# Finer pieces at the opening of an 8x8 max-pool-and-subtract kernel on Trainium2

## Chip, cores, metric

The kernel runs on one core of one Trainium2 chip. The metric is the device time of one execution, in microseconds, lower being better. Of seven executions of the kernel before, the median was 628.34 us (628.24 to 628.9).

## What is computed

The input `x` is float32 of shape 8 x 64 x 256 x 256 (134.22 MB). Each image is cut into blocks of 8 by 8 elements; from every element the maximum of its block is subtracted. The output has the shape of the input.

```python
x_r = x.reshape(B, C, oH, pH, oW, pW)          # pH = pW = 8
pooled = x_r.max(axis=(3, 5))
upsampled = np.repeat(np.repeat(pooled, pH, axis=2), pW, axis=3)
return (x - upsampled).astype(np.float32)
```

## The kernel before

One "row" here is eight image lines of one channel, 8 x 256 = 2048 float32 (8 KB): a row holds 32 whole blocks, and so every row can be worked on alone. There are 8 x 64 x 32 = 16,384 rows, 128 for each of the 128 partitions. The list `TILES` (L11) says how these 128 rows per partition are divided: 32 tiles of four rows each. Inside a tile a partition's rows stand next to each other in HBM (L69, L70), so a piece of one, two or four rows is one stretch of 8, 16 or 32 KB per partition, and 1, 2 or 4 MB over all partitions.

An entry of `TILES` is a pair of lists: the pieces in which a tile is loaded, and the pieces in which it is worked on and stored. Before, the first tile is loaded as two pieces of two rows and stored as two pieces of two rows; thirty tiles are loaded and stored as one piece of four rows; the last tile is loaded as one piece and stored as two, one and one rows.

For each tile the loop of L64 takes a buffer `dat` of 32 KB per partition (L65, from a pool of `BUFS` = 6 buffers) and a small one, `pooled`, for the maxima (L66). Then:

- each load piece is a DMA from `in_x_dram` into a slice of `dat`, issued from the SyncE queue (SP, L75);
- for each store piece VectorE (DVE) makes one TENSOR_REDUCE that takes the maxima of the piece's blocks into `pooled` (L41 where the piece has one row, L48 where it has more), then one TENSOR_TENSOR per row that subtracts them in place (L55), and then a DMA from `dat` to `out_dram` is issued from the ScalarE queue (ACT, L81).

All loads go through SP's DMA queue (q1 in the profile), all stores through ACT's (q10); both run on the same 16 DMA engines. TensorE is not used, and ScalarE and SyncE only issue DMAs. The order on each engine is the program's order (`manual_schedule`, L62). The waits come from the tile framework: DVE waits for the load piece it reads; a store waits for DVE; a load into a buffer used before waits until the stores of the tile six places earlier have landed. The DMAs signal on eight semaphores handed out in turn, so that a DMA also waits for the earlier DMA which has the same semaphore.

Of the kernel before, what the change touches and what calls it, by code (L numbers as in the profile page):

```python
# [1 line left out]

# [4 lines left out]

F32 = mybir.dt.float32
ROW = 2048

TILES = [([2, 2], [2, 2])] + [([4], [4])] * 30 + [([4], [2, 1, 1])]  # L11
BUFS = 6


@with_exitstack
def kernel(
    ctx: ExitStack,
    tc: tile.TileContext,
    x: bass.AP,
    out: bass.AP,  # L20
):
    nc = tc.nc
    P = nc.NUM_PARTITIONS
    B, C, H, W = x.shape
    pH = pW = 8
    oW = W // pW

    x_rows = x.rearrange("b c (oh ph) w -> (b c oh) (ph w)", ph=pH)
    out_rows = out.rearrange("b c (oh ph) w -> (b c oh) (ph w)", ph=pH)
    assert sum(sum(loads) for loads, _ in TILES) * P == x_rows.shape[0]  # L30
    size = max(sum(loads) for loads, _ in TILES)

    data = ctx.enter_context(tc.tile_pool(name="data", bufs=BUFS))
    small = ctx.enter_context(tc.tile_pool(name="small", bufs=BUFS))

    def pool_and_subtract(dat, tops, R):

        wins = dat.rearrange("p (r ph ow pw) -> p r ph ow pw", r=R, ph=pH, ow=oW)
        tops = tops.rearrange("p (r ow) -> p r ow", r=R)
        if R == 1:  # L40
            nc.vector.tensor_reduce(  # L41
                out=tops[:, 0],
                in_=wins[:, 0].rearrange("p ph ow pw -> p ow ph pw"),
                axis=mybir.AxisListType.XY,
                op=mybir.AluOpType.max,
            )
        else:
            nc.vector.tensor_reduce(  # L48
                out=tops,
                in_=wins.rearrange("p r ph ow pw -> p r ow ph pw"),  # L50
                axis=mybir.AxisListType.XY,
                op=mybir.AluOpType.max,
            )
        for r in range(R):
            nc.vector.tensor_tensor(  # L55
                out=wins[:, r],
                in0=wins[:, r],
                in1=tops[:, r].unsqueeze(1).unsqueeze(3).to_broadcast([P, pH, oW, pW]),
                op=mybir.AluOpType.subtract,
            )  # L60

    ctx.enter_context(tc.manual_schedule())  # L62
    at = 0
    for loads, stores in TILES:  # L64
        dat = data.tile([P, size * ROW], F32, name="dat")  # L65
        pooled = small.tile([P, size * oW], F32, name="pooled")  # L66

        rows = sum(loads)
        src = x_rows[at : at + P * rows].rearrange("(p r) d -> p (r d)", r=rows)  # L69
        dst = out_rows[at : at + P * rows].rearrange("(p r) d -> p (r d)", r=rows)  # L70
        at += P * rows
        lo = 0
        for R in loads:
            part = slice(lo * ROW, (lo + R) * ROW)
            nc.sync.dma_start(out=dat[:, part], in_=src[:, part])  # L75
            lo += R
        lo = 0
        for R in stores:
            part = slice(lo * ROW, (lo + R) * ROW)
            pool_and_subtract(dat[:, part], pooled[:, lo * oW : (lo + R) * oW], R)  # L80
            nc.scalar.dma_start(out=dst[:, part], in_=dat[:, part])  # L81
            lo += R


# [1 line left out]
_INS = ['x']  # L86
_OUTS = [((8, 64, 256, 256), 'float32')]


# [23 lines left out]
```

## Time and profile before

| | |
|---|---|
| median of seven executions | 628.34 us |
| the profiled execution, its own time | 628.47 us |
| span from its first to its last instruction | 626.5 us |
| moved from and to HBM | 134.22 MB read, 134.22 MB written |
| mean rate over the span | 428 GB/s |
| VectorE | 562.6 us busy (90% of the span), 163 instructions |
| DMAs: loads | 31 of 4096 KB, 2 of 2048 KB |
| DMAs: stores | 30 of 4096 KB, 3 of 2048 KB, 2 of 1024 KB |
| TENSOR_REDUCE of four rows, two rows, one row (mean) | 8.685, 4.418, 2.278 us |
| TENSOR_TENSOR of one row (mean) | 2.287 us |

The profile is of one execution. 1.97 us of its time lie outside the span. Times inside it count from the start of the span. "DMA" in tables of windows is the mean busy share of the 16 DMA engines, and GB/s what they moved, reads and writes together; a packet is counted where it begins, so that short windows scatter around the true share.

### The profile page before, as it was taken

Reading aid. Unit: us, or ns where it says so; the run is one execution under the profiler, and the core shown is the slowest. Engines: PE = TensorE matmul, PEld = TensorE weight load, DVE = VectorE, ACT = ScalarE, POOL = GpSimd, SP = SyncE. Lnnn points to the kernel's source line nnn. Section 1 sums busy time; section 2 is a strip of 40 time slices with the busy share of each in tenths; the row PEclk is TensorE's granted clock in tenths of the full one; section 3 lists DMA queues with packets and bytes.
Section 4 is the critical chain, followed back from the end, with each engine's and each line's share of the span. In section 5 each row is a group of like instructions: output and inputs, shape, how many; then the busy total and the mean of one; then the engine's idle time right before and its main releaser. Section 6 shows DMA issues by size and latency. Waiting matters only on the chain.

```text
span 626.5 us, 364 instructions
## 1 busy us (share of the span) xinstructions
DVE 562.6 (90%) x163; POOL 0.2 (0%) x4
## 2 busy tenths in 40 slices
DVE  4999999998898888988889988889888898888982
POOL 0000000000000000000000000000000000000000
DMA  9999999999999999999999999999999999999997
GB/s 370 400 446 425 435 435 435 435 435 435 435 435 431 433 435 429 429 429 427 435 435 433 435 435 435 435 435 435 435 435 433 433 435 427 431 423 433 435 434 337
DMA packets 9794, 268.46 MB, mean 428 GB/s; under 512 B 1088, under 2 KB 1088, under 8 KB 1088
## 3 DMA queue, kind: packets, MB, share of 16 engines
q1 hardware_dynamic: 4752, 134.22, 49.9%
q10 hardware_dynamic: 5040, 134.22, 49.6%
q14 instruction: 2, 0.02, 0.0%
HBM read 134.22 MB, written 134.22 MB: 428 GB/s over the span
## 4 chain that ended last, share of the span: by engine, by line
DVE 90%; another core or an unknown queue 7%; DMA 1%; issue 0%
DVE dat L55 45%; DVE pooled L48 44%; DMA dat<-in_x_dram 1%; DVE pooled L41 1%
## 5 line engine op out<-in xcount | busy, mean ns | idle before, releaser
L48 DVE TENSOR_REDUCE pooled<-dat 128x128 f32<-128x8192 f32 (+1 forms) x33 | 273.8, 8297 | 51.3 <-DMA dat<-in_x_dram 51.3
L55 DVE TENSOR_TENSOR dat<-dat,pooled 128x2048 f32<-128x2048 f32 x128 | 285.0, 2287 | 1.2
L41 DVE TENSOR_REDUCE pooled<-dat 128x32 f32<-128x2048 f32 x2 | 4.6, 2278 | 0.0
L97 POOL MEMSET const-bfloat16-1.0<- 128x1 bf16 x1 | 0.1, 102 | 0.0
L97 POOL MEMSET const-uint8-127<- 128x1 uint8 x1 | 0.1, 102 | 0.0
L97 POOL MEMSET const-float32-1.0<- 128x1 f32 x1 | 0.1, 99 | 0.0
L97 POOL MEMSET const-float32-0.0<- 128x1 f32 x1 | 0.1, 98 | 0.2 <-issue 0.2
## 6 DMA issues: line engine op xcount, KB each, us to landing
dat<-in_x_dram SPq DMA_DIRECT2D x31, 4096.0 KB, 60.9
out_dram<-dat ACTq DMA_DIRECT2D x30, 4096.0 KB, 37.5
out_dram<-dat ACTq DMA_DIRECT2D x3, 2048.0 KB, 19.9
dat<-in_x_dram SPq DMA_DIRECT2D x2, 2048.0 KB, 9.5
out_dram<-dat ACTq DMA_DIRECT2D x2, 1024.0 KB, 11.2
```

The costliest lines, as they stand in the source:

```text
L41: nc.vector.tensor_reduce(out=tops[:, 0], in_=wins[:, 0].rearrange("p ph ow pw -> p ow ph pw"), axis=mybir.AxisListType.XY, op=mybir.AluOp ...
L48: nc.vector.tensor_reduce(out=tops, in_=wins.rearrange("p r ph ow pw -> p r ow ph pw"), axis=mybir.AxisListType.XY, op=mybir.AluOpType.max,)
L55: nc.vector.tensor_tensor(out=wins[:, r], in0=wins[:, r], in1=tops[:, r].unsqueeze(1).unsqueeze(3).to_broadcast([P, pH, oW, pW]), op=mybir ...
L97: nc = _bacc.Bacc("TRN2", target_bir_lowering=False, num_devices=1)
```

## The change

One line: the first tile is now loaded and stored in pieces of one, one and two rows; the second tile, which came in as one piece of four rows and left as one, is now loaded and stored in two pieces of two rows (as the first tile was before); 29 whole tiles instead of 30 follow, and the last tile is as it was.

```diff
-TILES = [([2, 2], [2, 2])] + [([4], [4])] * 30 + [([4], [2, 1, 1])]
+TILES = [([1, 1, 2], [1, 1, 2]), ([2, 2], [2, 2])] + [([4], [4])] * 29 + [([4], [2, 1, 1])]
```

The built programs show what this makes of each engine's instructions. SP issues two loads of 1024 KB, three of 2048 KB and 30 of 4096 KB, 35 in place of 33. ACT issues two stores of 1024 KB, three of 2048 KB and 29 of 4096 KB ahead of the last tile's three, 37 in place of 35. DVE opens with two one-row reductions (L41), each with its subtraction, then three two-row reductions (L48) with two subtractions each, where it had two two-row reductions and one of four rows: two reductions more, and the same number of subtractions. The semaphores handed out in turn fall on other DMAs: in the program before, the sixth and the seventh load wait for the landing of the first and the third load; in the changed one the sixth to the ninth load wait for the first, third, fourth and fifth. The buffers, the engines that issue and everything after the second tile are unchanged.

## Prediction

> **What bounds the kernel now.** I read the page first: busy shares, rates by slice, DMA queues.
>
> ```profile
> DVE 562.6 (90%) x163; POOL 0.2 (0%) x4
> ...
> DVE  4999999998898888988889988889888898888982
> ...
> DMA  9999999999999999999999999999999999999997
> GB/s 370 400 446 425 435 435 435 435 435 435 435 435 431 433 435 429 429 429 427 435 435 433 435 435 435 435 435 435 435 435 433 433 435 427 431 423 433 435 434 337
> DMA packets 9794, 268.46 MB, mean 428 GB/s; under 512 B 1088, under 2 KB 1088, under 8 KB 1088
> ```
>
> DVE has holes in nearly every slice behind the first quarter; the DMA engines are at nine tenths or more from the first slice on, the last one apart. The rate stands at 423 to 435 GB/s whatever DVE does. That is a full pipe, with the time set by bytes. The chain of waits seems to say otherwise, so it was read second, together with DVE's and SP's waits:
>
> ```profile
> DVE 90%; another core or an unknown queue 7%; DMA 1%; issue 0%
> ...
> DVE pooled L48 <- DMA dat<-in_x_dram: 51.3, 26, 8.0
> ...
> SPq L75 <- DMA out_dram<-dat: 501.4, 27, 19.7
> SPq L75 <- DMA dat<-in_x_dram: 21.3, 2, 16.3
> ```
>
> The chain runs along DVE because it is followed from instruction to instruction; but DVE itself waits 26 times for a load, 8.0 us at the start and 43.3 us in the other 25. The 7% named as unknown are mostly these waits, some 1.72 us before each whole tile. So DVE keeps step with the loads, and the loads with the full pipe. Third, windows, to find where the pipe is not full:
>
> ```profile
> 0.00:2.00 2.00, 0.00 (x0) 0.20 (x4) 1.00 0.47 98
> 2.00:4.00 2.00, 0.00 (x0) 0.00 (x0) 1.00 0.75 295
> 4.00:12.00 8.00, 3.97 (x1) 0.00 (x0) 1.00 0.99 426
> 12.00:18.00 6.00, 5.96 (x4) 0.00 (x0) 1.00 1.01 437
> 18.00:24.00 6.00, 5.96 (x3) 0.00 (x0) 1.00 0.98 350
> 24.00:60.00 36.00, 35.93 (x11) 0.00 (x0) 1.00 1.01 437
> 120.00:580.00 460.00, 417.61 (x121) 0.00 (x0) 1.00 1.00 433
> 613.00:619.00 6.00, 2.16 (x1) 0.00 (x0) 1.00 0.93 396
> 619.00:623.00 4.00, 0.00 (x0) 0.00 (x0) 1.00 1.01 428
> 623.00:625.00 2.00, 0.00 (x0) 0.00 (x0) 1.00 0.17 70
> ```
>
> (The last column is GB/s.) I take 433, the long window, as the full rate: 268.46 MB need 620.0 us of the 626.5. The missing 6.5 us lie at the start (0 to 4 us moved 0.79 MB, worth 1.8 us: 2.2 lost), at 18 to 24 us (350 instead of 433: 6 x 83/433 = 1.15 lost, at a DMA share of 0.98, so packets were slow there, not absent) and behind 613 (0.5, then 0.05, then 3.2 us from 623 to the end); the 437s give some 0.4 back. In between nothing is to be had. Loads alone, from 4 to 18 us, run at the same rate as loads and stores together: a store that begins earlier does not fill an empty pipe, it takes turns with a load.
>
> **The change, part by part.** *An earlier first result.* These lines show the start and the end before:
>
> ```profile
> 8.03 4.42 DVE L48 TENSOR_REDUCE pooled<-dat 128x64 f32<-128x4096 f32 x1 [8.03 <-DMA dat<-in_x_dram]
> 12.48 4.49 DVE L55 TENSOR_TENSOR dat<-dat,pooled 128x2048 f32<-128x2048 f32 x2
> ...
> 17.01 44.26 ACTq L81 DMA_DIRECT2D out_dram<-dat  x4
> ...
> 612.86 2.29 DVE L55 TENSOR_TENSOR dat<-dat,pooled 128x2048 f32<-128x2048 f32 x1
> ```
>
> The first load of 2.10 MB is there at 8.03 us. Half of it saves 1.05 MB / 433 = 2.4 us, so the first row is there at 5.6 (an estimate). DVE then needs 2.28 + 2.29 = 4.57 us a row: first store at 10.2 instead of 17.0, second at 14.8. Two rows take 8.9 us (4.42 + 4.49): stores at 23.7, 32.6 and 41.5 us. The second tile ends at 41.5 where it ended at 43.3 (25.75 + 8.68 + 8.90, less overlap): DVE is 1.8 us ahead. On the path this is worth 0: DVE waits 43.3 us for loads later on, and its lead goes into the next of those waits.
>
> *What the earlier stores displace.* From 10.2 to 17.0 us the pipe was full of loads. At an equal share of bytes the stores take at most half of these 6.8 us: loads run up to 3.4 us later from then on. What would be late next is the end. DVE's last subtraction ended at 615.15 us (612.86 + 2.29); its store of 1.05 MB needs 2.4 us, and the pipe was busy with older stores until 623 to 625. So the last row waited some 5 to 7 us for the pipe, and 3.4 us later is still soon enough: 0. The trace speaks for less than that. The page counts 9794 packets; 68 DMAs of 128 partitions and 16 marks under 512 B each (1088 in all) make 9792, so a packet is one partition's piece. If the queues take turns packet by packet, stores of 8 and 16 KB pass beside loads of 16 and 32 KB at a third of the pipe. Then the eight opening rows, where four were small before, let the loads get further ahead instead of falling behind. Either way the order of the work changes, not its amount.
>
> [...]
>
> *More, smaller packets.* The nearest row for one-row pieces is 619 to 623 us, where one-row stores alone run at 428 against 433. Four pieces of one row (two loads, two stores) are 4.19 MB: 9.80 instead of 9.69 us, +0.11. Two-row pieces rise from four to six in the opening, 4.19 MB more, and the nearest row is 4 to 12 us, two-row loads at 426: +0.15. The marks of four more DMAs are below 0.05. I take +0.3. The lower end is 0 (12 to 18 us shows 437). No row has one-row loads; the upper end is the 396 GB/s of 613 to 619, where the pieces shrink: 8.4 MB at 396 costs 1.8 us more than at 433.
>
> [...]
>
> *The dip when stores join.* The 1.15 us at 18 to 24 us begin just behind the issue of the first store at 17.01. They do not come back at the second one, issued in the 24 to 60 us window (437). I take the dip to come once, earlier: change 0. The ends: it is gone (-1.15), or doubled (+1.15).
>
> *Instructions added.* DVE: 2 x 2.278 - 4.418 = 0.14 us more in the first tile, 2 x 4.418 - 8.685 = 0.15 in the second; hidden by its waits of 43.3 us, and were those gone, 0.3. SP and ACT issue two DMAs more each, 0.33 to 0.49 us an issue by the trace. SP's fall into the first 3 us, when each piece passes in 2.4 us or longer, so SP stays ahead. On ACT nothing but stores is behind them.
>
> *Semaphores and buffers.* Four loads (sixth to ninth) now wait for an earlier load instead of two. Before, two such waits took 21.3 us of SP and the pipe stayed full. The sixth load waits until 5.6 us, with 7.3 MB (17 us) queued ahead; the ninth waits for the fifth, with three tiles queued. Behind them on SP are only later loads. The first load that reuses a buffer (seventh tile) waits for three stores of the first tile, done by 45 us even at a third of the pipe; by then some 14 MB of 25 are loaded, so it comes over 20 us early. Whole loads took 60.9 us to land where 19.4 pass for a tile: they are queued some 40 us ahead, and that cover is not used up. Cost 0; without it, up to 19.7 us a tile, SP's longest wait.
>
> **Sum.** 626.5 span + 1.97 around it = 628.47; + 0.3 = 628.8 for a run like the profiled one. That run stands 0.13 above the median, so 628.6.
>
> **The rivals.** *DVE's lead reaches the end* (faster). The chain of waits is 90% DVE, and DVE begins 2.4 us earlier. If that were handed through, 628.34 - 2.4 = 626.0. Against it: DVE idles in front of 25 tiles, and the last stores queue. With the dip gone as well it is the only way below -0.2%. 8%.
>
> *The store queue runs dry between one-row pieces* (slower). DVE makes a row in 4.57 us; alone the pipe passes it in 2.4, at half share in 4.8. If stores pass faster than at half share, the queue empties after the first piece, and each new piece joins anew and pays the dip: up to four more joins, 4.6 us; I take half, 2.3, so 628.3 + 0.3 + 2.3 = 630.9. It decides from one extra join (1.15 + 0.3 is over 0.2%). For it: only 0.3 us of margin at equal shares. Against it: the first store came out slowly, landing 19.9 us after issue (median of three two-row stores), which leaves room for the second to queue. 13%, with one-row loads at the slow bound in it.
>
> *No change to speak of* (my forecast): 628.6. 79%.
>
> **How the numbers follow.** About 0.2%, 1.26 us, is what a measurement of this kernel tells from no change, so "same" is 627.1 to 629.6, and the three cases are the three chances. The range: 627.3 is the forecast without the dip; upward, a dip doubled and small pieces halfway to their bound give 628.6 + 1.15 + 0.6 = 630.3. About 2 in 10 lie outside.
>
> **What would show it.** Right: first reduction (L41) at 5 to 6 us, first store issued near 10, second tile done near 41.5, one window of low rate between 10 and 18 us, 433 GB/s from 24 us on, DVE waiting 1.7 us a tile, and stores draining for 5 us or more behind DVE's last subtraction. Wrong: a second dip before 45 us, an SP wait that leaves the DMA share under 0.97, or the span ending right behind DVE.

## The result, and the profile after

Sixteen executions of the changed kernel had a median of 630.63 us, from 627.86 to 640.82; 42 of the kernel before, run beside them, a median of 628.3, from 628.02 to 628.9. The ratio is 1.0036, 95% interval 1.0025 to 1.0047: slower by 0.36%. The spread says more than the median: these 42 executions of the kernel before lie within 0.9 us, while the changed kernel is in some executions faster than any of them and in others 12 us slower. (Each ratio here and below leaves out executions over 1.5% above the same kernel's fastest, here 637.47, 639.39 and 640.82, of which the first is the profiled one.) The kernel before is not wholly free of late executions either: of 73 more, run beside the experiments below, one took 632.72 us and the other 72 at most 628.69. A second profile, of an execution from the middle of the spread, is therefore read beside the first.

Parts of the page, for the slices and rates, of the execution of 637.47 us:

```profile
span 635.4 us, 372 instructions
...
DVE  6999999998889888899888898888988889888891
...
DMA  9999999999999999999999999999999999999993
GB/s 361 432 431 427 428 441 439 435 429 429 429 429 430 441 439 433 433 429 429 427 429 439 439 435 431 429 429 429 429 433 431 439 439 427 429 429 429 435 406 138
DMA packets 10371, 268.46 MB, mean 422 GB/s; under 512 B 1152, under 2 KB 1152, under 8 KB 1152
```

Nothing in it looks like a stall: the pipe is at nine tenths or more until the last slice. But that slice moves 138 GB/s where it moved 337. The same execution by windows (share of the DMA engines, then GB/s, in the last columns) shows what it is:

```profile
120.00:580.00 460.00, 411.88 (x120) 0.00 (x0) 1.00 1.00 432
...
620.00:624.00 4.00, 2.29 (x1) 0.00 (x0) 1.00 0.68 285
...
626.00:634.00 8.00, 0.00 (x0) 0.00 (x0) 1.00 0.06 27
```

A share of 0.06 is one engine in sixteen. For the last eight microseconds a single DMA engine works alone, at its full rate (27 GB/s is a sixteenth of 433). Fifteen are done. DVE's steps show the same engine; the timeline of this execution, from its opening and from late in the run, with the wait and its cause in brackets:

```profile
5.61 2.29 DVE L41 TENSOR_REDUCE pooled<-dat 128x32 f32<-128x2048 f32 x1 [5.61 <-DMA dat<-in_x_dram]
...
10.26 31.44 ACTq L81 DMA_DIRECT2D out_dram<-dat  x5
...
36.83 4.49 DVE L55 TENSOR_TENSOR dat<-dat,pooled 128x2048 f32<-128x2048 f32 x2
41.84 8.69 DVE L48 TENSOR_REDUCE pooled<-dat 128x128 f32<-128x8192 f32 x1 [0.52 <-DMA dat<-in_x_dram]
...
484.33 8.69 DVE L48 TENSOR_REDUCE pooled<-dat 128x128 f32<-128x8192 f32 x1 [2.31 <-DMA dat<-in_x_dram]
...
504.39 8.69 DVE L48 TENSOR_REDUCE pooled<-dat 128x128 f32<-128x8192 f32 x1 [2.44 <-DMA dat<-in_x_dram]
...
524.43 8.69 DVE L48 TENSOR_REDUCE pooled<-dat 128x128 f32<-128x8192 f32 x1 [2.42 <-DMA dat<-in_x_dram]
```

The opening is as the change has it, and as it was worked out. But late in the run the tiles come every 20.05 us. Before, they came every 19.36, with waits of 1.74:

```profile
558.42 8.69 DVE L48 TENSOR_REDUCE pooled<-dat 128x128 f32<-128x8192 f32 x1 [1.74 <-DMA dat<-in_x_dram]
...
577.78 8.69 DVE L48 TENSOR_REDUCE pooled<-dat 128x128 f32<-128x8192 f32 x1 [1.74 <-DMA dat<-in_x_dram]
```

Each load ends with 16 marks on its semaphore, and DVE begins when the last of them has come (the last load's 15th mark comes at 593.97, its 16th at 604.30, and DVE begins on it at 604.33); these marks stand in the trace one by one. Here they are for some loads of this execution, in us, tiles counted from one:

```
load of   first mark   median   15th     16th
tile 6      87.09       88.35    88.75    89.66
tile 10    164.58      165.84   166.20   169.26
tile 16    280.76      282.01   283.36   286.19
tile 22    397.01      398.20   400.00   404.67
tile 28    513.43      514.37   516.41   524.40
tile 32    590.88      591.82   593.97   604.30
last store 626.05      626.12   626.22   634.61
```

The 16th mark falls behind the 15th by 0.9 us at the sixth tile and by 10.3 at the last, some 0.36 us a tile, and the end of the kernel is the end of that engine. In the trace of before the 16 marks of the load that lands at 558.40 lie within 1.35 us. The second profile of the changed kernel (span 628.1) shows the same in small: last store's 15th mark at 625.00, 16th at 627.28.

Where the late engine loses its time was read from the trace's packet records. They do not name the engine, but on one engine each packet begins where the one before it ended, so that the packets of the late engine can be followed. "L" is a 32 KB load packet, "S" a store packet, "L-end" and "S-end" the marks that end a DMA; the plain packets take 1.21 us:

```
S 482.74 | L-end 483.95 | S 483.96 | L 485.17, took 1.89 | S-end 487.05 | L 487.06 | S 488.27 | L 489.48 ...
S 502.78 | L-end 503.99 | S 504.00 | L 505.21, took 1.71 | S-end 506.92 | L 506.92 took 1.39 | S 508.31 ...
```

It alternates, one load packet, one store packet, and never idles. But in this part of the run the first packet of each new load is long, and a store ends just one turn (one load packet and one store packet) behind the load's end.

### The profile page after: what moved, and what is told of

It reads as the page before. It is cut to its first block, busy times and chain, and to the rows that moved or that the text cites. A ratio compares the mean times of both kernels' runs of the same rounds, so it can differ in the third digit from the quotient of the medians.

```text
span 635.4 us, 372 instructions
## 1 busy us (share of the span) xinstructions
DVE 562.9 (89%) x165; POOL 0.2 (0%) x4
## 2 busy tenths in 40 slices
DMA packets 10371, 268.46 MB, mean 422 GB/s; under 512 B 1152, under 2 KB 1152, under 8 KB 1152
## 4 chain that ended last, share of the span: by engine, by line
DVE 83%; another core or an unknown queue 8%; DMA 6%; issue 0%
DVE dat L55 42%; DVE pooled L48 40%; DMA dat<-in_x_dram 6%; DVE pooled L41 1%
## 5 line engine op out<-in xcount | busy, mean ns | idle before, releaser
L48 DVE TENSOR_REDUCE pooled<-dat 128x128 f32<-128x8192 f32 (+1 forms) x33 | 269.5, 8168 | 52.5 <-DMA dat<-in_x_dram 52.5
L41 DVE TENSOR_REDUCE pooled<-dat 128x32 f32<-128x2048 f32 x4 | 9.1, 2282 | 5.6 <-DMA dat<-in_x_dram 5.6
```

Of the source, the lines that this page charges most:

```text
L41: nc.vector.tensor_reduce(out=tops[:, 0], in_=wins[:, 0].rearrange("p ph ow pw -> p ow ph pw"), axis=mybir.AxisListType.XY, op=mybir.AluOp ...
L48: nc.vector.tensor_reduce(out=tops, in_=wins.rearrange("p r ph ow pw -> p r ow ph pw"), axis=mybir.AxisListType.XY, op=mybir.AluOpType.max,)
```

## The experiments

Seen in numbers that need no engine's name: the 32 KB load packets after 60 us that took over 12 ns longer than the usual 1.213 us. Before there is one of them among 3546; in the changed kernel's first profile 101, losing 14.8 us of engine time together, in the second 43, losing 4.1.

**The theory of turns (Theory D in the expectations)** was formed after the first four runs, and their results are told with it. In the changed kernel's first profile 72 DMAs of 128 packets and 16 marks make 10,368 of the page's 10,371 packets. Followed from one to the next there, 1047 of the 1080 stretches between two marks of one queue have 8 packets, whether these are of 8 KB (0.31 us each), 16 KB (0.61) or 32 KB (1.21). If load and store packets take strict turns as soon as both queues hold work, every DMA lasts eight turns, and the number of turns by which a store's end lies behind a load's end never changes again: it is fixed by the packet of a load at which the first store joins. The packets agree: from 60 to 560 us, 7422 of the 7423 packets and marks of the kernel before, and 7479 of 7484 in the changed kernel's first profile, have one of the other queue that begins within 0.01 us of their end. A turn is two packets, 2.42 us in the steady part, so the place can be read off as the distance of the load's and the store's median marks.

The packet records allow more than the median: with each packet linked to the one of the other queue that begins where it ends, all 16 engines can be followed from 60 to 560 us in each profile. In all 13 profiles the number of engines in each place is the same wherever it was counted between these times. In the kernel before, ten engines are two turns ahead and six one turn. In the changed kernel, in both profiles, nine engines are two turns behind, six three turns, and one, the late one, a single turn. Up to 590 us of its first profile, that one engine's long load packets lose 10.7 us, against 1.8 us for the nine together and 1.7 us for the six; in the second profile it is 2.3 us against 1.1 and 0.2.

**First: which part of the change does it?** Theory A, held at first: one-row stores. The changed kernel was run again (after_again).

> The changed kernel once more, for its spread and a second profile. In its first profile 15 of the 16 load marks of a tile land within 3 us of each other and the 16th up to 10 us later, by steps of about 0.3 us a tile. Theory (one DMA engine falls behind, by an amount that differs between executions): times from about 628 to 640 again, median 630 to 632, and in this profile the last mark again late, by about as much as the span exceeds 625.8. Rival (the slow times were a disturbed chip): all within 628.0 to 629.0, like the kernel before.

Measured: 630.02 us (627.94 to 639.68, 11 runs), ratio 1.0018 (1.0002 to 1.0035). The spread comes again; the span exceeds 625.8 by 2.3 and the 16th mark of the last store is late by 2.3. Not a disturbed chip.

The next diffs are against the kernel before. They all replace the same line, which only the first of them shows. In first_only the first tile alone is cut:

```diff
-TILES = [([2, 2], [2, 2])] + [([4], [4])] * 30 + [([4], [2, 1, 1])]
+TILES = [([1, 1, 2], [1, 1, 2])] + [([4], [4])] * 30 + [([4], [2, 1, 1])]
```

> Only the first tile is cut into one, one and two rows; the second is whole as before. Theory A (one-row stores that join a stream of larger loads set an engine behind): spread like the changed kernel's, median 630 to 632, over 628.9 in most runs. Theory B (the cut second tile is needed for it): like before, all within 628.0 to 629.0.

Measured: 643.74 us, ratio 1.024 (1.0226 to 1.0253), far over both expectations. All 16 engines are one turn behind. Four runs lie within 642.9 to 644.1, two more at 677.9 and 679.1, which nothing here explains. By windows, the page's full pipe is full and yet slower:

```profile
100.00:580.00 480.00, 426.50 (x122) 0.00 (x0) 1.00 1.00 423
```

615 load packets are long, losing 171.7 us of engine time, 10.7 us for each of 16 engines. Seen by the turns: one of its loads has its median mark at 108.92 and the next store at 111.36, 2.4 us or one turn behind; the changed kernel has 88.35 and 93.51, a little over two turns, as nine engines at two and six at three make it.

In second_only it is the second tile alone:

```diff
+TILES = [([2, 2], [2, 2])] * 2 + [([4], [4])] * 29 + [([4], [2, 1, 1])]
```

> Only the second tile is cut into two and two rows; the first stays at two and two. Theory A: no one-row piece, so like before, 628.0 to 629.0. Theory B (more two-row stores beside four-row loads, and the larger lead of the loads over the stores, set an engine behind): spread like the changed kernel's, median 630 or more.

Measured: 628.08 us (627.95 to 628.36), ratio 0.9997 (0.9988 to 1.0005). Theory B falls. One long load packet; the store's median mark 174.61, the load's 181.78, three turns ahead.

In loads_only the loads alone come in the pieces of the change:

```diff
+TILES = [([1, 1, 2], [2, 2]), ([2, 2], [4])] + [([4], [4])] * 29 + [([4], [2, 1, 1])]
```

> The loads of the first two tiles come in the changed kernel's pieces, the stores leave in the pieces of before. Theory A (the stores do it): like before, 628.0 to 629.0. Rival C (the smaller load pieces do it, whichever way the rows leave): spread to 634 or more, median 630 or more. If both loads and stores are needed, also like before.

Measured: 628.55 us (628.13 to 629.14), ratio 1.0005 (0.9996 to 1.0013). One run, 629.14, lies just above the expected 629.0; the median does not, and Rival C falls. Two turns ahead (166.53 against 171.43), one long packet, as before.

In their direction all four go with theory A, too, though A says neither why first_only is so much slower than the changed kernel nor why a cut second tile makes 643.7 into 630. The next experiments set A against the turns.

**Second: one-row stores, or the place at which they join?** The delay used from here on is work for DVE alone: reductions over half a row into a spare tile, ahead of the first reduction, each 1.22 us. The first kernel, stores_only, has no delay; its stores alone leave in the pieces of the change:

```diff
+TILES = [([2, 2], [1, 1, 2]), ([4], [2, 2])] + [([4], [4])] * 29 + [([4], [2, 1, 1])]
```

> The stores of the first two tiles leave in the changed kernel's pieces, the loads come in the pieces of before. Theory A (one-row stores beside larger loads set engines behind): spread, median 630 or more. Theory D (turn theory: loads and stores take strict turns on each DMA engine, eight turns to a DMA whatever its piece, so the place in a load at which the first store joins fixes for the whole run how many turns a store's end lies behind a load's end; one turn behind is the slow place, as in the kernel with only the first tile cut, where the marks lie 2.4 us apart): first store issued near 12.6 us, joining near 16.2, about three 32 KB packets (1.21 us each) into the load that began at 12.0; three turns behind, so 628.0 to 629.0.

Measured: 627.89 us (627.84 to 628.06), ratio 0.9987 (0.9972 to 1.0001). All the small stores of the change, and no long run. Marks at 116.37 and 123.59: three turns, as expected of the turns; the store joined at 17.16 instead of 16.2. Theory A falls.

The delay is added like this, here twice:

```diff
+DELAY = 2
...
+    spare = ctx.enter_context(tc.tile_pool(name="spare", bufs=1)).tile([P, oW], F32, name="spare")
...
         lo = 0
+        for _ in range(DELAY if at == P * rows else 0):
+            nc.vector.tensor_reduce(
+                out=spare,
+                in_=dat[:, : ROW // 2].rearrange("p (ph ow pw) -> p ow ph pw", ph=pH // 2, ow=oW),
+                axis=mybir.AxisListType.XY,
+                op=mybir.AluOpType.max,
+            )
         for R in stores:
```

With the pieces of before and two such reductions (before_late2):

> The kernel before, with two redundant half-row reductions (2.3 to 2.4 us of DVE together, written to a spare tile) ahead of its first reduction; pieces and loads unchanged. Theory A (no one-row piece in the opening) and DVE's slack of 43 us: 628.0 to 629.0. Theory D: the first store joins two 32 KB packets later; before, the store ends one turn ahead of the load's end on 6 engines and two ahead on 10, so these go to one turn behind and level; with engines one turn behind it is slow: 630 to 645, and engines late at the end.

Measured: 630.81 us (629.79 to 634.77), ratio 1.0048 (1.003 to 1.0065). The profiled execution is the slowest of them, 634.77. Nine engines are level (median marks 130.18 and 130.72), seven one turn behind. 323 load packets are long by 40.4 us, nearly all on the seven, and here store packets, too: 840 of them, 70.7 us, of which 64.4 lie on the nine. So the level place costs something of its own, about 7 us an engine in this execution. With three (before_late3):

> As before, with three redundant half-row reductions (3.5 us). Theory A: 628.0 to 629.0. Theory D: three packets later, so one and two turns behind; the larger part of the engines at one turn behind: 635 to 650, like the kernel with only the first tile cut.

Measured: 643.78 us (643.14 to 643.98), ratio 1.0244 (1.0229 to 1.0259). All 16 engines are one turn behind (128.45 and 130.87), where Theory D had expected only the larger part of them there; 585 load packets are long. The kernel before, with no piece changed, made as slow as the slowest cut by 3.7 us of work in an engine that otherwise idles for 43. Its opening in the timeline, and its steady part by windows:

```profile
8.06 3.73 DVE L81 TENSOR_REDUCE spare<-dat 128x32 f32<-128x1024 f32 x3 [8.06 <-DMA dat<-in_x_dram]
...
20.67 0.38 ACTq L90 DMA_DIRECT2D out_dram<-dat  x1
```

```profile
100.00:580.00 480.00, 431.07 (x122) 0.00 (x0) 1.00 1.00 423
```

And the slow cut of the first tile, with two reductions (first_late2):

> Only the first tile cut into one, one and two rows (643.7 us as it is), with two redundant half-row reductions (2.3 to 2.4 us of DVE) ahead of its first reduction. Theory A (one-row pieces do it): 640 or more, as without them. Theory D: the first store joins two 32 KB packets later, three turns behind instead of one: 628.0 to 629.5, faster by 15 although DVE does more.

Measured: 627.83 us (627.75 to 628.35), ratio 0.9993 (0.9983 to 1.0002). Three turns (106.54 and 113.76), 8 long load packets. Its opening and its steady part:

```profile
5.55 2.47 DVE L81 TENSOR_REDUCE spare<-dat 128x32 f32<-128x1024 f32 x2 [5.55 <-DMA dat<-in_x_dram]
...
12.57 13.71 ACTq L90 DMA_DIRECT2D out_dram<-dat  x3
```

```profile
100.00:580.00 480.00, 442.28 (x126) 0.00 (x0) 1.00 1.00 434
```

2.4 us of useless work took 15.9 us away. 434 against 423 GB/s at the same share of 1.00 is the whole of it.

**Third: the changed kernel itself, DVE's part, and a candidate for a better version.** The changed kernel with one half-row reduction (after_late1):

> The changed kernel, all its pieces kept, with one redundant half-row reduction (1.2 us of DVE) ahead of its first reduction. Theory D (strict turns; slow where a store's end lies one turn behind a load's end): the first store joins about two 16 KB packets (0.61 us each) later; the 15 engines that were two turns behind go to four, the one that was one turn behind to three: no spread, all runs 627.7 to 628.5. Theory A (the one-row pieces): 628 to 640 as before.

Measured: 628.04 us (627.54 to 628.16), ratio 0.9994 (0.9985 to 1.0003), 2 long load packets, four turns (86.18 and 95.70) on ten engines; one run, 627.54, lies below the expected 627.7. (The expectation took fifteen engines of the changed kernel to be at two turns; by the packets nine are, and six at three.) All of the change's pieces are there, and the loss is gone. So the small pieces by themselves do not cost it.

The slow kernel before_late3, with DVE's work left out behind the eighth tile (late3_nodve):

```diff
-            pool_and_subtract(dat[:, part], pooled[:, lo * oW : (lo + R) * oW], R)
+            if at <= 8 * P * size:
+                pool_and_subtract(dat[:, part], pooled[:, lo * oW : (lo + R) * oW], R)
```

> The kernel before with three redundant half-row reductions (one turn behind, 643.8 us), and from the ninth tile on maxima and subtractions left out: these rows are stored as they were loaded. Theory D, DMA alone: loads and stores in the same places, so 638 to 646 although DVE does a quarter of its work. Rival E (DVE's reduction, which starts when the last load mark has landed, disturbs the load packets beside it): 627 to 629.

Measured: 643.38 and 641.01 us, ratio 1.0221 (1.0202 to 1.0239); one turn (128.68 and 131.11), 629 long load packets. From 100 to 580 us, by windows:

```profile
100.00:580.00 480.00, 52.02 (x15) 0.00 (x0) 1.00 1.00 424
```

DVE is all but silent there, and the pipe is as slow. The loss is between the two DMA queues; DVE only sets when the first store joins.

The cut of the stores alone, again (stores_again):

> The kernel with the stores of the first two tiles cut and their loads as before, again, as the candidate that beats both: three turns behind on all engines. Theory D: 627.8 to 628.1 in every run, 0.05 to 0.1% under the kernel before, no late runs.

Measured: 627.96 us (627.8 to 628.03, 11 runs), ratio 0.9993 (0.9984 to 1.0002). It beats the changed kernel clearly and stands 0.35 us under the kernel before, with no late run in 21; the interval does not exclude that it is equal to that one.

The places, together (turns from the load's end to the store's end, with the number of engines in each place; the places and the long packets are those of the profiled execution):

| kernel | turns (engines) | long load packets | median us |
|---|---|---|---|
| second_only | 3 ahead (11), 2 ahead (5) | 1 | 628.08 |
| loads_only | 3 ahead (2), 2 ahead (14) | 1 | 628.55 |
| before | 2 ahead (10), 1 ahead (6) | 1 | 628.3 |
| before_late2 | level (9), 1 behind (7) | 323 | 630.81 |
| first_only; before_late3; late3_nodve | 1 behind (16) | 615; 585; 629 | 643.74; 643.78; 642.19 |
| changed kernel (two profiles) | 1 behind (1), 2 behind (9), 3 behind (6) | 101; 43 | 630.63 |
| stores_only | 3 behind (16) | 1 | 627.89 |
| stores_again | 2 behind (1), 3 behind (14), 4 behind (1) | 1 | 627.96 |
| first_late2 | 2 behind (2), 3 behind (12), 4 behind (2) | 8 | 627.83 |
| after_late1 | 3 behind (5), 4 behind (10), 3 ahead (1) | 2 | 628.04 |

## Why the prediction was wrong

It forecast no change, 628.6 us, and gave 630.3 as the upper end; the median is 630.63 and the ratio's interval lies above 1.0025. The rival on the slower side named 630.9, near the measured time, but by a mechanism that did not happen.

*Right.* The opening went as worked out: first reduction at 5.61 (5.6 in the sum), first store at 10.26 (10.2), second tile done at 36.83 + 4.49 = 41.3 (41.5). DVE's lead is worth nothing, as said: it goes into waits for loads (behind the first, 25 waits of 45.2 us together in the second profile, where it was 25 of 43.3). Semaphore waits cost nothing: SP waited 23.4 us for loads in four waits, and the pipe stayed full (shares of 1.00 and 1.01 in the windows below). The store queue did not run dry: the first store's last packet ended at 21.35, the second had been issued at 14.78. The dip at the joining of the stores came once and earlier, as said (396 GB/s from 10 to 18 us), and the windows behind it show no second one of its size:

```profile
10.00:18.00 8.00, 7.97 (x4) 0.00 (x0) 1.00 1.00 396
18.00:24.00 6.00, 5.96 (x4) 0.00 (x0) 1.00 1.01 430
24.00:60.00 36.00, 35.38 (x12) 0.00 (x0) 1.00 1.01 431
```

*The size of the small pieces.* +0.3 us was too much, by all that was seen. after_late1 has every piece of the change and stands at 0.9994 (0.9985 to 1.0003); the changed kernel's own fastest executions end at 627.9 to 628.1. A slip in the range: the forecast of 628.6 without the dip of 1.15 is 627.45, not 627.3; it decides nothing here.

*The step that failed* is the sentence "Either way the order of the work changes, not its amount", for which the sum has no term. Two things in it do not hold. The 16 engines were added up into one pipe, with a mean rate of 433; but the kernel ends with its slowest engine, and in the changed kernel's profile the mean from 120 to 580 us is still 432 while one engine loses some 10 us. And the order does change the amount: the same packets take longer where the store's end comes one turn behind the load's end, up to 1.92 us in place of 1.21 in the changed kernel's first profile, and up to 2.52 in before_late3. I had both halves in hand, the turns by packets and the earlier joining of the first store, and asked of them only who gets ahead, loads or stores, not where in the eight turns they meet. The trace of before could not have priced it, since on none of its engines a store ends one turn behind (ten are two turns ahead and six one turn).

*How the change came to it.* Its first store joins at 13.90 us instead of 21.00, in a load of 16 KB packets that began at 11.99, two or three packets in. That puts nine engines two turns and six three turns behind, which costs next to nothing (1.8 us for the nine and 1.7 for the six together, in the first profile), and one engine, whose load marks come a packet later (89.66 against 88.35), one turn behind. How late that engine ends differs between executions: with one engine in the slow place in both profiles, its long load packets lose 10.7 us in one and 2.3 us in the other. No execution without a late engine was profiled. It can be that in these no engine lands in the slow place, or that one does and loses little; no run here tells which.

*What stays open* is why this place is slow. It is not DVE (late3_nodve, 642.19 us), and not the size of the pieces (after_late1, 628.04). The long packets stand where one queue begins a DMA while the other ends one. One turn behind, most are among the first three packets of a new load (in first_only from 60 to 560 us, 145, 159 and 135 of 684 long packets, with 142 of the 164 us lost), and the end mark of the store comes right behind the first of them (at 487.05, behind the packet that began at 485.17, in the lines of the changed kernel above). In the level place, where a load and a store end together (130.18 and 130.72 in before_late2), they are mostly store packets, which lose 64.4 us on the nine engines there. What makes packets long in these places, no run here tells.

## What to carry to other kernels

Where two DMA queues keep the pipe full (here loads on one, stores on the other), a mean share of 1.00 does not show that it is at its best (here it stood beside 423 GB/s and beside 434): compare the time from tile to tile with the bytes at the best rate seen, look at the spread of the 16 marks of one DMA, and at a last window with a share near 0.06. The moment at which the second queue joins can fix a pattern for the whole run (here from 60 to 560 us in all 13 profiles; with 3.7 us of DVE's work ahead of its first store, the kernel before took 643.78 us in place of 628.4), so try a delay of one, two and three packets in the opening before judging a change to it. And run it more than ten times: a spread of 12 us, where 42 executions of the kernel before had one of 0.9, is the result, more than the median.

## What the hardware showed that was not expected

Eight turns to a DMA, whether its packets are 8, 16 or 32 KB (8 packets in 1047 of 1080 stretches), and a distance between loads and stores that stays, on every engine that could be followed, from 60 to 560 us. With all 16 engines in one of the eight places the kernel takes 2.4% longer (643.78 us, ratio 1.0244); with nine engines in its neighbour on one side and seven in the slow place itself, 0.5% (630.81); its neighbour on the other side cost the nine engines there 1.8 us together. The 16 engines of one DMA can end far apart: in the last load of the changed kernel's first profile 10 us lie between the 15th and the 16th mark, at 593.97 and 604.30, and DVE began on it only at 604.33.
